# A two-layer hybrid transformer block: where the first feed-forward block of each stage puts its weights

## The chip, the cores and the metric

One core of a Trainium2 chip runs the whole kernel as one launch. The metric is the time of one execution on the device, in microseconds (us). TensorE is written PE, VectorE DVE, ScalarE ACT, GpSimd POOL and the engine that issues most of the DMAs SP.

## The reference

The input is 256 tokens of width 2048, in float32. Two layers follow each other. Layer 0 mixes with a gated delta rule and a gated linear recurrence, layer 1 with two kinds of attention; each mixer ends in an output projection that is added to the residual `h`. After each mixer comes the same feed-forward part, and the change is in it:

```
def swiglu(hn, w_gate, w_up, w_down):
    return (jax.nn.silu(hn @ w_gate) * (hn @ w_up)) @ w_down

def reference(...):
    h = x
    for layer in range(DEPTH):                      # 2
        h = h + mixer(rmsnorm(h, ...), ...)
        h = h + swiglu(rmsnorm(h, ffn_norm[layer]), ffn_w_gate[layer], ffn_w_up[layer], ffn_w_down[layer])
    return rmsnorm(h, final_norm)
```

`w_gate` and `w_up` are 2048 x 5632, `w_down` is 5632 x 2048.

## The kernel before, in words

Float32 products are made of two rounded halves. A weight tile `raw` of 128 x 1024 floats (512 KB) comes from memory; ACT casts it to the high half (`whi` or `thi`, line 608 in the feed-forward part, line 181 in the mixers), DVE subtracts that from `raw` and gets the low half (`wlo` or `tlo`, line 620, in the mixers line 182). PE then multiplies with the high and low halves of the activations `X`: high by high, high by low, low by high (lines 473 to 475).

There are four phases: mixer 0, feed-forward 0, mixer 1, feed-forward 1. Each phase opens pools of its own with `phase()` (lines 65 to 75), over the memory of the phase before. A tile in them can be written only when all that the earlier phase still reads in that memory is done. Pools `wr` (three buffers for `raw`), `wh` (four for `whi`), `wl` (three for `wlo`) and the accumulators in `acc` and `msp` stay through all phases. The phase's own `mx` pool gives further buffers for weights, two under each of the names `raw`, `ha`, `hb` and `hc`; its `fp` pool gives `thi` and `tlo` (two of each) and `comb`.

`ffn()` (line 720) cuts the work into blocks, eleven for the hidden columns (512 of gate and of up each) and six for the way down, and each block into steps (class `Step`, line 438). A plain step (`simple`, line 480) loads one 512 KB tile and uses it in 12 matmuls of 128 x 512. Other steps belong to a scheme with seven products in place of eight (`seven`, line 490); it holds tiles in `ha`, `hb`, `hc` and adds further weights to them with accumulating DMAs from POOL. The first block of each stage has no such products: it is sixteen plain steps, called step 0 to step 15 here. Steps with odd number use another pair of accumulators (F01, F11) than those with even number (F00, F10).

`stream()` (line 566) writes the steps out. `loads_to` (577) issues loads up to eight steps ahead as long as a buffer under the wanted name is promised free; `ahead` (597) writes the casts, `low` (615) the subtractions. Every sixth cast from step 1 and from step 4 goes to `thi`; the subtractions of steps 1 and 3 of every five go to `tlo`. What is written is then ordered for each engine by the framework's scheduler by when operands and buffers become free, up to the first step of the second block, from which the written order is kept (`guard`, line 628). SP issues the loads of all phases in one order: a load whose buffer isn't free holds back all behind it.

In the kernel before, the first ten steps of a stage ask in turn for `raw`, `ha`, `raw`, `hb`, `raw`, `hc` (lines 486 to 488), and of the loads that ask for `raw`, the first, third, sixth and so on get a buffer of the new `mx` pool and the others one of `wr` (line 592). Step 0 so loads to a new buffer, step 1 to `ha`, step 2 to `wr`.

Ahead of the stage stands the mixer's output projection (`xstat`, lines 305 to 307; `out_proj`, 356). After its last matmuls DVE adds the result to `h` in two halves of 128 tokens (line 361), ACT sums the squares of `h` into a scrap tile `junk` of the old mixer's memory (line 319), PE transposes `h` (line 328), ACT and DVE make the two halves of the last quarter of `X` (329, 330).

Of the kernel before, what the change touches and what calls it, by code (L numbers as in the profile page):

```python
# [4 lines left out]
F32, F32R, I32 = dt.float32, dt.float32r, dt.int32  # L5
# [42 lines left out]
def body(tc, A, out):  # L48
# [8 lines left out]
    wr = pool("wr", 3)  # L57
# [4 lines left out]
    mx, ogp, fp = Phase(), Phase(), Phase()  # L62
# [91 lines left out]
    def tick():  # L154

        count[0] += 1
        if paused[0]:
            return
        n = 0
        odd = not more and count[0] % 2  # L160
        for t in list(tasks)[::turns[0]]:
            if count[0] - t[0] >= t[2] and n < (2 if more else 4) and not (odd and t[2] > 1):
                step(t)
                n += 1
# [280 lines left out]
    class Mix:  # L445
# [34 lines left out]
        def simple(self, i, u, first):  # L480
            b = {}

            def use(w, tt=(0, 1)):
                for t in tt:
                    self.add(t, i, lambda kk: self.xs(2 * u + kk, t), w)
            k = 2 * u + i
            return Step(("raw", "ha", "raw", "hb", "raw", "hc")[k % 6] if first and k < 10 else "raw",
                        lambda raw: nc.sync.dma_start(raw, self.src(i, u)), use, unit=(i, use))

        def seven(self, m):  # L490
# [75 lines left out]
    def stream(order, puts, guard):  # L566

        at = [0, 0, 0]
        where = {id(y): k for k, y in enumerate(order)}
        g = None

        slots, count_raw = {}, [0]

        def loads_to(n, must=False):
            while at[2] < min(n, len(order)):
                y = order[at[2]]
                if y.tag:  # L580
                    q = slots.setdefault(y.tag, [])
                    if len(q) == (5 if y.tag == "raw" else 2):
                        k = where[id(q[0])]
                        if k >= at[1]:
                            if not must:
                                return
                            low(k)
                        q.pop(0)
                    q.append(y.free)
                    if y.tag == "raw":  # L590
                        count_raw[0] += 1
                    y.raw = (wr.tile([128, 1024], F32, name="raw") if y.tag == "raw" and count_raw[0] % 5 in (0, 2, 4) else
                             mx.tile([128, 1024], F32, name=y.tag, tag=y.tag, bufs=2))
                    y.load(y.raw)
                at[2] += 1

        def ahead(n):

            while at[0] < min(n + 1, len(order)):
                y, k = order[at[0]], at[0]  # L600
                loads_to(k + 1, True)
                for z in y.needs:
                    low(where[id(z)])
                if y.ready:
                    y.raw = y.ready()
                y.hi = (fp.tile([128, 1024], F32R, name="thi", tag="thi", bufs=2) if k % 6 in (1, 4) else
                        wh.tile([128, 1024], F32R, name="whi"))
                S.copy(y.hi, y.raw)  # L608
                at[0] += 1
                if at[0] > 1:  # L610
                    low(at[0] - 2)
            while at[1] < min(n, len(order)):
                low(at[1])

        def low(k):
            while at[1] <= k:
                y, j = order[at[1]], at[1]
                y.lo = (fp.tile([128, 1024], F32R, name="tlo", tag="tlo", bufs=2) if j % 5 in (1, 3) else
                        wl.tile([128, 1024], F32R, name="wlo"))
                V.tensor_sub(y.lo, y.raw, y.hi.bitcast(F32))  # L620
                at[1] += 1
                if y.after:
                    y.after()

        for n, y in enumerate(order):
            for f in puts.get(n, []):
                f()
            if y is guard:
                g = tc.manual_schedule(engines={V.engine, S.engine, PE.engine})
                g.__enter__()  # L630
            loads_to(n + 8)
            ahead(n + 1 + 3)
            y.use((y.hi, y.lo))
            if y.unit:
                tick()
        for n in sorted(k for k in puts if k >= len(order)):
            for f in puts[n]:
                f()
        if g is not None:
            g.__exit__(None, None, None)  # L640
# [79 lines left out]
    def ffn(L, then, fin=None):  # L720
# [120 lines left out]
        else:  # L841
            put(q + 2, lambda: then(0), lambda: then(1))
        stream(order, puts, blocks[1].early[0])

        if not fin:
# [757 lines left out]
```

## Time and profile before

| | |
|---|---|
| median of 3 runs | 2230.15 us (2229.86 to 2231.21) |
| the profiled execution | 2229.7 us |
| its span, first to last instruction | 2227.5 us |
| PE busy | 2203.5 us (99%) |
| DVE busy | 1829.3 us (82%) |
| ACT busy | 1341.4 us (60%) |
| DMA | 485.25 MB, 218 GB/s on average |
| mean granted PE clock | 0.996 |

The profile is one execution. "PE F L473 <- ACT whi L608" names an engine, what it wrote and the line, and who released it. In the chain of waits, the program is followed back from its last instruction, at each step to what released it, so its rows join end to start. In a timeline, the first column is the start in us from the span's start, the second the duration; a matmul's duration overlaps the next one's start, so the pace of PE is read from the starts. "SPq" is SP's queue of DMA issues. In the answers on DMAs the last column is the time from issue to landing.

### The profile page before, as it was taken

How to read it: one execution, taken by the hardware profiler on the slowest of the kernel's cores; microseconds unless marked ns; L12 is line 12 of the kernel's file. 1: busy time of each engine (PE TensorE's matmuls, PEld its weight loads, DVE VectorE, ACT ScalarE, POOL GpSimd, SP SyncE). 2: the span in 40 equal slices, each digit the busy share in tenths (PEclk: the TensorE clock that was granted, in tenths of full speed). 3: DMA queues.
4: the chain of work that ended last, by engine and by line, in shares of the span. 5: the costliest groups of instructions: out<-in, count | busy, mean ns of one | idle time of the engine just before them, and what ended most of it. 6: DMA issues, size and time to landing. Idle time of an engine off the chain costs nothing.

```text
span 2227.5 us, 30574 instructions
## 1 busy us (share of the span) xinstructions
PE 2203.5 (99%) x10960; PEld 1844.0 (83%) x10960; DVE 1829.3 (82%) x2554; ACT 1341.4 (60%) x1775; POOL 106.2 (5%) x126
## 2 busy tenths in 40 slices
PE   9999999999999999999999999999999999999998
PEld 8888888788888888888888888887888888888886
DVE  8899676679888888888786688857888888988886
ACT  6776664556665666666654554445665566665665
POOL 0000000000100000000000000000000100100000
PEclk9999999999999999999999999999999999999999
DMA  7445446687988888888555455566788887888884
GB/s 285 156 146 166 139 149 187 206 256 228 257 267 247 237 284 237 264 255 253 171 188 158 156 186 171 162 184 221 219 255 277 237 274 245 238 272 249 234 263 133
DMA packets 135209, 485.25 MB, mean 218 GB/s; under 512 B 15088, under 2 KB 16624, under 8 KB 134928
## 3 DMA queue, kind: packets, MB, share of 16 engines
q1 hardware_dynamic: 117488, 420.10, 54.6%
q0 software_dynamic: 17280, 62.92, 16.4%
q8 instruction: 86, 1.41, 0.3%
q14 instruction: 67, 0.55, 0.1%
q10 hardware_dynamic: 288, 0.27, 0.0%
HBM read 481.13 MB, written 2.10 MB: 217 GB/s over the span
## 4 chain that ended last, share of the span: by engine, by line
PE 97%; DVE 1%; DMA 1%; ACT 0%; issue 0%; DVEq 0%; ACTq 0%; SPq 0%
PE F L474 20%; PE F L473 20%; PE F L475 20%; PE Pw L201 11%; PE Pw L206 6%; PE Px L305 3%; PE Px L306 3%; PE Px L307 3%; PE F L420 1%; PE F L421 1%; PE Ph L735 1%; PE F L419 1%; PE Psc L1365 1%; PE Pw L247 0%; PE Pt L328 0%; PE Pw L248 0%
## 5 line engine op out<-in xcount | busy, mean ns | idle before, releaser
L181 ACT CAST whi<-raw 128x1024 fp32r<-128x1024 f32 x245 | 256.8, 1051 | 266.3 <-PE Pw L201 86.4
L182 DVE TENSOR_TENSOR wlo<-raw,whi 128x1024 fp32r<-128x1024 f32 x245 | 298.8, 1220 | 118.7 <-PE Px L306 37.7
L201 PE MATMUL Pw<-X,whi 128*128 128x512 f32 x1088 | 388.4, 400 | 0.0
L608 ACT CAST whi<-raw 128x1024 fp32r<-128x1024 f32 x238 | 249.4, 1054 | 109.9 <-PE F L475 88.1
L206 PE MATMUL Pw<-X,wlo 128*128 128x256 f32 x1088 | 304.8, 280 | 0.1
L473 PE MATMUL F<-whi,X 128*128 128x512 f32 x712 | 279.2, 393 | 9.9 <-ACT whi L608 9.9
L475 PE MATMUL F<-whi,X 128*128 128x512 f32 x712 | 278.2, 391 | 0.0
L608 ACT CAST whi<-ha 128x1024 fp32r<-128x1024 f32 x152 | 160.5, 1056 | 167.0 <-DVE ha L503 41.4
L201 PEld LDWEIGHTS Pw<-X,whi 128*128 128x128 f32 x1088 | 204.2, 188 | 47.2 <-issue 0.5
L474 PE MATMUL F<-wlo,X 128*128 128x512 f32 x588 | 230.4, 392 | 0.1
L206 PEld LDWEIGHTS Pw<-X,wlo 128*128 128x128 f32 x1088 | 205.4, 189 | 1.5 <-DVE wlo L182 0.7
L620 DVE TENSOR_TENSOR wlo<-raw,whi 128x1024 fp32r<-128x1024 f32 x140 | 170.3, 1219 | 4.6 <-ACT whi L608 0.9
L473 PEld LDWEIGHTS F<-whi,X 128*128 128x128 f32 x712 | 134.4, 189 | 37.9 <-ACT whi L608 10.4
L474 PE MATMUL F<-tlo,X 128*128 128x512 f32 x420 | 163.4, 389 | 0.0
L475 PEld LDWEIGHTS F<-whi,X 128*128 128x128 f32 x712 | 134.4, 189 | 27.9
L620 DVE TENSOR_TENSOR wlo<-ha,whi 128x1024 fp32r<-128x1024 f32 x96 | 117.4, 1222 | 37.4 <-ACT whi L608 25.6
L608 ACT CAST thi<-ha 128x1024 fp32r<-128x1024 f32 x92 | 97.3, 1057 | 76.4 <-DVE ha L503 32.6
L474 PEld LDWEIGHTS F<-wlo,X 128*128 128x128 f32 x588 | 111.2, 189 | 24.4 <-DVE wlo L620 1.5
L473 PE MATMUL F<-whi,hid 128*128 128x512 f32 x336 | 131.2, 390 | 0.0
L475 PE MATMUL F<-whi,hid 128*128 128x512 f32 x336 | 130.8, 389 | 0.0
L608 ACT CAST thi<-raw 128x1024 fp32r<-128x1024 f32 x100 | 105.2, 1052 | 36.7 <-PE F L475 32.1
L474 PE MATMUL F<-wlo,hid 128*128 128x512 f32 x320 | 124.5, 389 | 0.0
(444 smaller groups left out, 4887.8 us busy)
## 6 DMA issues: line engine op xcount, KB each, us to landing
raw<-in_gu SPq DMA_DIRECT2D x222, 512.0 KB, 5.5
raw<-in_dn SPq DMA_DIRECT2D x116, 512.0 KB, 4.9
raw<-in_w0w SPq DMA_DIRECT2D x72, 512.0 KB, 3.7
raw<-in_wo SPq DMA_DIRECT2D x64, 512.0 KB, 3.7
raw<-in_w1w SPq DMA_DIRECT2D x64, 512.0 KB, 3.7
ha<-in_gu SPq DMA_DIRECT2D x44, 512.0 KB, 5.2
hb<-in_gu SPq DMA_DIRECT2D x44, 512.0 KB, 7.6
hc<-in_gu SPq DMA_DIRECT2D x42, 512.0 KB, 5.6
```

Of the source, the lines that this page charges most:

```text
L181: S.copy(hi, raw)
L182: V.tensor_sub(lo, raw, hi.bitcast(F32))
L201: PE.matmul(P.rearrange("p a b -> p (a b)"), hi[:, kk], X[:, k].rearrange("p a b -> p (a b)"), start=k == 0, stop=False)
L206: PE.matmul(P[:, 0], lo[:, kk], X[:, k, 0], start=False, stop=k == NK - 1)
L305: PE.matmul(Ps[t], x[:, 0, ts], hi[:, kk], start=k == 0, stop=False)
L306: PE.matmul(Ps[t], x[:, 0, ts], lo[:, kk], start=False, stop=False)
L307: PE.matmul(Ps[t], x[:, 1, ts], hi[:, kk], start=False, stop=k == n - 1)
L473: PE.matmul(P, xh, hi[:, kk], start=z[0] == 1 and kk == 0, stop=False, skip_group_check=skip)
L474: PE.matmul(P, xh, lo[:, kk], start=False, stop=False, skip_group_check=skip)
L475: PE.matmul(P, xl, hi[:, kk], start=False, stop=kk == 1 and z[0] in z[1:], skip_group_check=skip)
L608: S.copy(y.hi, y.raw)
L620: V.tensor_sub(y.lo, y.raw, y.hi.bitcast(F32))
```

## The change: what it does

All steps of a stage's first block now carry the name `first`, and such a load always gets one of the three `wr` buffers. Other plain loads take turns between `wr` and `mx` as before, with a counter of their own (`turn`), and the bookkeeping of promised buffers is kept for each pool of buffers apart (`wr` 3, and 2 each of `raw`, `ha`, `hb`, `hc`) rather than five for `raw` together. Nothing is computed otherwise, and each engine has the same instructions as before.

```diff
-            k = 2 * u + i
-            return Step(("raw", "ha", "raw", "hb", "raw", "hc")[k % 6] if first and k < 10 else "raw",
+            return Step("first" if first else "raw",
                         lambda raw: nc.sync.dma_start(raw, self.src(i, u)), use, unit=(i, use))
...
-        slots, count_raw = {}, [0]
+        slots, turn = {}, [0]
+        bufs = dict(wr=3, raw=2, ha=2, hb=2, hc=2)
...
-                    q = slots.setdefault(y.tag, [])
-                    if len(q) == (5 if y.tag == "raw" else 2):
+                    wide = y.tag == "raw" and turn[0] % 5 in (1, 3)
+                    tag = y.tag if wide or y.tag in bufs and y.tag != "raw" else "wr"
+                    q = slots.setdefault(tag, [])
+                    if len(q) == bufs[tag]:
...
-                    if y.tag == "raw":
-                        count_raw[0] += 1
-                    y.raw = (wr.tile([128, 1024], F32, name="raw") if y.tag == "raw" and count_raw[0] % 5 in (0, 2, 4) else
-                             mx.tile([128, 1024], F32, name=y.tag, tag=y.tag, bufs=2))
+                    turn[0] += y.tag == "raw"
+                    y.raw = (wr.tile([128, 1024], F32, name="raw") if tag == "wr" else
+                             mx.tile([128, 1024], F32, name=tag, tag=tag, bufs=bufs[tag]))
```

The line numbers below the first edit grow by one or two: the cast of line 608 stands in line 609 after the change, the subtraction of line 620 in line 621, the load of line 488 in 487, that of line 499 in 498.

The order of the instructions changes on every engine around the start of both feed-forward stages, in the same way at both. The three pieces below are from the first one.

SP, from the last loads of mixer 0's output projection on, before. L488 is a plain step's load, L499 one of the seven-product steps of the second block:

```order
L175 DMA raw<-in_wo 128x1024 x32
L488 DMA raw<-in_gu 128x1024 x4
L488 DMA ha<-in_gu 128x1024
L488 DMA hb<-in_gu 128x1024
L488 DMA raw<-in_gu 128x1024
L488 DMA hc<-in_gu 128x1024
L488 DMA ha<-in_gu 128x1024
L488 DMA hb<-in_gu 128x1024
L488 DMA raw<-in_gu 128x1024 x2
L499 DMA ha<-in_gu 128x1024
```

The same place on SP after the change (L487 a plain load, L498 one of the second block):

```order
L175 DMA raw<-in_wo 128x1024 x32
L487 DMA raw<-in_gu 128x1024 x5
L498 DMA ha<-in_gu 128x1024 x2
L498 DMA hb<-in_gu 128x1024
L487 DMA raw<-in_gu 128x1024 x3
L498 DMA hb<-in_gu 128x1024
L498 DMA hc<-in_gu 128x1024
L487 DMA raw<-in_gu 128x1024 x3
L498 DMA hc<-in_gu 128x1024
L487 DMA raw<-in_gu 128x1024 x3
```

Before, the first three loads go to `wr` (they are those of steps 2, 6 and 8), the fourth is step 0's, to the new memory. After, the first five are steps 0 to 4 in their order, all to `wr`, and three loads of the second block, to the new memory, stand ahead of step 5's.

ACT around the end of the mixer, before. The x4 at L329 make a quarter of `X`; `junk` is the sum of squares; L399 is a cast for the seven-product scheme:

```order
L181 CAST whi<-raw 128x1024 x2
L319 ACTIVATE junk,ssp<-h 128x512 x2
L329 ACTIVATE X<-Pt,col 128x256 x4
L319 ACTIVATE junk,ssp<-h 128x512 x2
L329 ACTIVATE X<-Pt,col 128x256 x4
L608 CAST whi<-raw 128x1024 x2
L608 CAST thi<-ha 128x1024
```

And after the change:

```order
L181 CAST whi<-raw 128x1024 x2
L319 ACTIVATE junk,ssp<-h 128x512 x2
L609 CAST whi<-raw 128x1024
L329 ACTIVATE X<-Pt,col 128x256 x4
L609 CAST whi<-raw 128x1024 x2
L319 ACTIVATE junk,ssp<-h 128x512 x2
L329 ACTIVATE X<-Pt,col 128x256 x4
L609 CAST thi<-raw 128x1024 x2
L399 CAST comb<-cc_4740 128x1024
```

Three casts, those of steps 0, 2 and 3, moved ahead of the last sum of squares; step 1's and step 4's, to `thi`, follow the last quarter of `X`. DVE's subtractions of steps 0 and 2 moved in the same manner ahead of the last additions to `h`.

PE at the same place, before. F_4654 and F_4661 are the accumulators F00 and F10:

```order
L307 MATMUL Px_4489<-whi,Od 128x512
L328 MATMUL Pt<-tab,h 128x128 x8
L473 MATMUL F_4654<-whi,X 128x512
L473 MATMUL F_4661<-whi,X 128x512
L474 MATMUL F_4654<-wlo,X 128x512
L475 MATMUL F_4654<-whi,X 128x512
```

And after the change, where F00 is F_4648:

```order
L307 MATMUL Px_4489<-whi,Od 128x512
L473 MATMUL F_4648<-whi,X 128x512
L328 MATMUL Pt<-tab,h 128x128 x4
L474 MATMUL F_4648<-wlo,X 128x512
L328 MATMUL Pt<-tab,h 128x128 x4
L475 MATMUL F_4648<-whi,X 128x512
L473 MATMUL F_4648<-whi,X 128x512
```

Step 0's matmuls now start between the mixer's last matmul and the eight last transposes. Behind step 0 come two matmuls of step 2, then two of step 1, six of step 2, ten of step 1 and four of step 2, and then step 3, 4, 5 and so on in turn.

## The prediction

> **What bounds the kernel now.** I read the busy times, then the chain that ended last, then PE's waits.
>
> ```profile
> PE 2203.5 (99%) x10960; PEld 1844.0 (83%) x10960; DVE 1829.3 (82%) x2554; ACT 1341.4 (60%) x1775; POOL 106.2 (5%) x126
> PE 97%; DVE 1%; DMA 1%; ACT 0%; issue 0%; DVEq 0%; ACTq 0%; SPq 0%
> PE F L473 <- ACT whi L608: 9.9, 2, 5.0
> ```
>
> PE is busy 99% of the span and carries 97% of the chain. Little is left to win, 24 us of idle time, and 9.9 us of that are two waits of 5 us for a cast. They stand at the two starts of the feed-forward part, where the change is. The chain through the first start, and the load in the chain at the second:
>
> ```profile
> 429.91 0.24 PE Px L307
> ...
> 430.17 0.70 DVE h L361
> ...
> 430.96 0.64 ACT junk L319 x2
> ...
> 431.64 0.72 ACT junk L319 x2
> ...
> 432.39 3.56 DMA raw<-in_gu
> ...
> 436.03 1.05 ACT whi L608
> ...
> 437.12 1.22 PE F L473 x2
> ```
> ```profile
> 1523.79 3.74 DMA raw<-in_gu
> ```
>
> The mixer's last matmul is followed by the addition to `h`, the sum of squares into `junk`, a load of 3.56 us, a cast of 1.05 us, and only then step 0's matmuls. The load has to wait for `junk` because its buffer lies in memory that the mixer still uses. The granted clock, in stretches from the end of the mixer's last matmul on:
>
> ```profile
> 430.67:437.12 6.45, 1.46 (x9) 0.76 0.59 191
> 437.12:440.88 3.76, 3.71 (x8) 0.51 1.02 416
> 1522.07:1528.70 6.63, 1.45 (x9) 0.82 0.57 187
> 1528.70:1533.27 4.57, 4.53 (x10) 0.52 1.01 407
> ```
>
> After the gap PE runs for 3.8 and 4.6 us at a clock of 0.51 and 0.52 (fifth column). So each start costs an idle stretch and a slow one. How long the start takes as a whole is read from PE's timeline:
>
> ```profile
> 423.87 0.39 PE L306 MATMUL Px<-wlo,Od 128*128 128x512 f32 x1
> ...
> 427.48 0.39 PE L306 MATMUL Px<-wlo,Od 128*128 128x512 f32 x1
> ...
> 430.43 0.39 PE L307 MATMUL Px<-whi,Od 128*128 128x512 f32 x1
> ...
> 444.62 0.39 PE L473 MATMUL F<-whi,X 128*128 128x512 f32 x1
> ...
> 447.34 0.39 PE L473 MATMUL F<-whi,X 128*128 128x512 f32 x1
> ...
> 1521.83 0.39 PE L307 MATMUL Px<-whi,Om 128*128 128x512 f32 x1
> ...
> 1539.24 0.39 PE L473 MATMUL F<-whi,X 128*128 128x512 f32 x1
> ```
> ```profile
> 424.49 0.87 PE Pt L328 x8
> ```
>
> A step is 12 matmuls; step 2 runs from 444.62 to 447.34, 2.72 us, 0.227 a matmul. The mixer's last matmul starts at 430.43 and is through at 430.66; step 3 starts at 447.34. That is 16.68 us for steps 0 to 2 and eight transposes. At the second start it is 1522.06 to 1539.24, 17.18 us. The work itself is 3 x 2.72 = 8.16 us and 0.87 us of transposes, 9.03 us. So 7.65 and 8.15 us are lost, 15.8 in all, and no more than that can be won here.
>
> **The change, first part: the loads start earlier.** SP's issues before:
>
> ```profile
> 417.42 0.33 SPq L488 DMA_DIRECT2D raw<-in_gu  x1
> 420.25 2.96 SPq L488 DMA_DIRECT2D raw<-in_gu  x2
> 432.39 0.33 SPq L488 DMA_DIRECT2D raw<-in_gu  x1
> ```
> ```profile
> raw<-in_gu SPq DMA_DIRECT2D x1, 512.0 KB, 3.5
> ```
>
> At 417.42, 420.25 and 422.88 (the end of the second row, less 0.33) the three `wr` buffers are refilled, with steps 2, 6 and 8. Now the same three issues bring steps 0, 1 and 2, and by 3.5 to 3.6 us each they are there at 421, 424 and 426.5. What ACT and DVE do around that:
>
> ```profile
> 424.74 1.57 ACT L329 ACTIVATE X<-Pt,col 128x256 fp32r<-128x256 f32 x4 [3.16 <-PE Pt L328]
> ...
> 432.27 1.55 ACT L329 ACTIVATE X<-Pt,col 128x256 fp32r<-128x256 f32 x4
> ...
> 437.93 1.04 ACT L608 CAST thi<-ha 128x1024 fp32r<-128x1024 f32 x1
> ```
> ```profile
> 421.63 1.23 DVE L182 TENSOR_TENSOR wlo<-raw,whi 128x1024 fp32r<-128x1024 f32 x1 [0.80 <-ACT junk L319]
> ...
> 430.17 1.37 DVE L361 TENSOR_TENSOR h<-Px,h 128x512 f32<-128x512 f32 x2 [3.27 <-PE Px L307]
> 432.40 1.23 DVE L407 TENSOR_TENSOR cf<-X 128x1024 f32<-128x1024 f32 x1 [0.85 <-ACT junk L319]
> 433.54 1.66 DVE L330 SCALAR_TENSOR_TENSOR X<-Pt,col,X 128x256 fp32r<-128x256 f32 x4
> 435.11 0.75 DVE L396 TENSOR_TENSOR cc<-cf 128x256 f32<-128x256 f32 x2
> ...
> 436.57 0.16 DVE L340 TENSOR_SCALAR rx<-rx 128x2 f32<-128x2 f32 x1
> ...
> 440.52 1.22 DVE L401 TENSOR_TENSOR comb<-cc,comb 128x1024 fp32r<-128x1024 f32 x1
> ```
>
> Step 0 is cast about 422 to 423, when the mixer's `whi` of four tiles back is free; its subtraction waits for `wlo` of three tiles back, whose last matmul (L306 at 423.87) ends at 424.3, and is done by 425.5. That frees the first buffer: step 3's load, issued at 425.6, lands at 429.2 and is cast by 430.3. Step 2 is cast by 427.6, ahead of `junk`, and subtracted when the mixer's next `wlo` falls free at 427.9 (L306 at 427.48), by 429.15. That frees the buffer for step 4, which lands at 432.8. All of it lies in idle time of ACT and DVE: ACT's 3.16 us before 424.74, DVE's 3.27 us before 430.17. It delays neither `h` at 430.17 nor `junk` at 430.96; the nearest thing is step 3's cast, with 0.6 us in hand.
>
> **Second part: PE's order.** Both halves of step 0 being there, PE goes from the mixer's last matmul at 430.66 into step 0's first one. The transposes of the first half need `h` at 430.87, those of the second at 431.54, and with a matmul between them each has only some 0.1 us to wait; so step 0 and the transposes end at 430.66 + 2.72 + 0.87 + 0.15 = 434.4. Two matmuls of step 2 follow, to 434.85. Step 1's high half goes to `thi`, in new memory, and so its cast can only follow `junk` and the last quarter of `X`: 432.27 + 1.55 = 433.8, and with 1.04 us of cast it is there at 434.85, just when PE asks for it. Its subtraction stands behind the last L330 on DVE, which ends at 435.1, and is done at 436.3; PE has two matmuls of step 1 and six of step 2 to do until 436.7. Steps 1 and 2 end at 434.4 + 2 x 2.72 = 439.88.
>
> **Third part: what is late next.** From step 3 on a load waits for the subtraction three steps back. DVE does steps 3 and 4 by 437.4 and 438.6, PE starts them at 439.88 and 442.6. Step 5's load waits for step 1's buffer until 436.3, and on SP it stands behind two `ha` and one `hb`, which have waited for `junk` until 432.39 as step 0's load did before. What a pile on the queue costs, from the seven loads that were issued between 432.39 and 435.52, is in the last column (the fourth and the last of them):
>
> ```profile
> raw<-in_gu SPq DMA_DIRECT2D x1, 512.0 KB, 6.8
> hb<-in_gu SPq DMA_DIRECT2D x1, 512.0 KB, 9.4
> ```
>
> The fourth, issued at 433.71, lands at 440.5, the seventh, at 435.52, at 444.9: 1.5 us for each load in the pile. Three loads from 432.4 on are through by 439, so step 5 lands at about 440.2 and its cast could be done at 441.3. On DVE, though, four operations on `cc` and two small ones (435.11 to 436.73, 1.6 us), one on `cf` (1.2) and one on `comb` (1.2) stand between step 4's subtraction and step 5's, so that this one ends at 438.6 + 4.0 + 1.2 = 443.8. PE asks for it with the second matmul of step 5, 439.88 + 5.44 + 0.23 = 445.55: 1.75 us in hand. By the same count step 8's low half is there at 451.8, needed at 453.7, step 11's at 457.9, needed at 461.9. No wait is left. The queue also carries the second block's tiles, but these are issued earlier than before.
>
> **The sum.** Steps 0 to 2 end at 439.88 and not at 447.34: 7.46 us. At the second start the same 9.22 us take the place of 17.18: 7.96 us. Together 15.4 us. In other terms: the idle time goes, 5.56 + 5.74 us (437.12 - 430.66 and 1528.70 - 1522.06, less 0.9 of transposes each), and so does what the low clock costs, 10.22 - 8.16 = 2.06 and 10.54 - 8.16 = 2.38 us, less 0.3 us of small waits. All that follows is bound by PE, so the gain should reach the end. The profiled execution, at 2229.7 us, becomes 2214.3; the median of the runs is 0.45 us above it, and the forecast is 2214.8 us.
>
> The slow stretch is the term that rests least on counting. The Trainium skill ("TensorE: Matmul & The Clock Gate", part "What's actually happening") says that PE falls to half its clock after an idle window of about 3.4 us and comes back after as long a busy one. By that the slow stretch costs half of 3.4 us, 1.7 us at each start, and the sum would be 14.4 us; the trace has 2.06 and 2.38, and I go by the trace.
>
> **Rivals.** *The ring of three is a little late.* If each of the loads of steps 5, 8 and 11 took as long as the median `hb`,
>
> ```profile
> hb<-in_gu SPq DMA_DIRECT2D x44, 512.0 KB, 7.6
> ```
>
> step 5's would land at 436.3 + 7.6 = 443.9, its low half would be there at 446.25 (0.7 us late), and each round of three steps would take 7.6 + 1.05 + 1.2 + 0.1 = 9.95 us of load, cast and subtraction against PE's 8.16: 1.8 us more at steps 8 and 11 each, some 4.2 us at each start. The gain would be 15.4 - 8.4 = 7 us, the time 2222 to 2223. For it speaks that the second block's loads share the queue; against, that they are few and lone loads take 3.5 us. Chance 0.14.
>
> *Slower: starvation.* The same ring becomes a loss where a load takes 8.8 us in each of three rounds (4.2 + 3 x 1.2 = 7.8 us at a start); at the 9.4 us of the row above it would be 4.2 + 5.4 = 9.6 us against a gain of 7.7, so 3.8 us slower in all, 2234; if the gaps pulled the clock down again, more. For: such a landing is in the trace, and SP is in order. Against: it belonged to seven loads issued in 3.6 us, and a ring of three can't pile up so. Chance 0.06.
> The Trainium skill's "DMA: Bandwidth & Descriptors" (part "Rules for kernel authors") speaks on this side: issue a DMA early and wait late, so that its fixed cost overlaps. Before, nine loads could be ahead; now three are, and no run here shows yet what that costs.
>
> *No change.* The new order could be held by something else that falls free only with `junk`, such as `thi`: step 1 stands in the sum with no time in hand. But even were all of PE to wait for it, steps 0 and 2 would be done meanwhile. Only if step 0 also waited until 437 would the time stay at 2230. Chance 0.04.
>
> **Numbers.** The forecast has 0.76: 2213.5 (all 15.8 us, and the runs' 0.7 us) to 2219 (up to 2 us lost again at each start). The range reaches into the first rival, to 2222. Faster by over 0.2% (4.5 us, about what a measurement of this kernel can tell from none) are the forecast and the first rival, 0.90; same 0.04; slower 0.06.
>
> **What would show it.** Right: the 9.9 us of PE's wait for the cast at its two places are gone, PE's clock stays at 1.0 there, and step 3 starts 9.2 us after the mixer's last matmul. Wrong: PE waits for L609 or L621 at steps 4 to 8, with landings of 7 us or more in the ring; or a wait for `thi` at step 1; or the gain is there at 450 us and gone at the second block.

## The result and the profile after

The changed kernel takes 2214.84 us (median of 4 runs, 2214.37 to 2215.07), the kernel before, run beside it, 2230.6 us (2229.86 to 2231.21). The ratio is 0.9929, 95% interval 0.9912 to 0.9946. The profiled execution took 2214.64 us, its span 2212.8 us.

The busy times and the shares of the chain, after:

```profile
PE 2198.9 (99%) x10960; PEld 1842.3 (83%) x10960; DVE 1827.9 (83%) x2554; ACT 1339.6 (61%) x1775; POOL 105.9 (5%) x126
PE 98%; DVE 1%; ACT 0%; DMA 0%; issue 0%; DVEq 0%; ACTq 0%
```

PE's waits, all that the view lists, after:

```profile
PE Pz L92 <- ACT tab L89: 2.7, 1, 2.7
PE Pgate L950 <- ACT cx L887: 0.6, 1, 0.6
PE Pt L328 <- DVE X L330: 0.4, 1, 0.4
```

The two waits of 5 us for a cast are gone and nothing has come in their place; what is left was there before. PE's timeline at the first start, after, from the mixer's last matmul to step 3's first one:

```profile
431.02 0.39 PE L307 MATMUL Px<-whi,Od 128*128 128x512 f32 x1
431.25 0.39 PE L473 MATMUL F<-whi,X 128*128 128x512 f32 x1
431.51 0.66 PE L328 MATMUL Pt<-tab,h 128*128 128x128 f32 x4
431.93 0.47 PE L474 MATMUL F<-wlo,X 128*128 128x512 f32 x1
432.24 0.61 PE L328 MATMUL Pt<-tab,h 128*128 128x128 f32 x4
...
435.43 0.64 PE L473 MATMUL F<-thi,X 128*128 128x512 f32 x2
...
440.43 0.39 PE L473 MATMUL F<-whi,X 128*128 128x512 f32 x1
```

And PE in the stretches of steps 0 to 2 at both starts, after (busy time, granted clock, share of the DMA engines, GB/s):

```profile
431.25:440.43 9.18, 9.18 (x45) 1.00 0.68 220
1514.86:1524.04 9.18, 9.18 (x46) 1.00 0.81 282
```

Step 0 follows the mixer's last matmul without a gap, and steps 0 to 2 with the eight transposes take 9.18 us at each start, at full clock, where they took 16.68 and 17.18 us. That is 7.50 + 8.00 = 15.5 us, against 15.8 us between the medians.

### The profile page after: what moved, and what is told of

Its sections match the earlier page's. It is cut to its first block, busy times and chain, and to the rows that moved or that the text cites. A ratio compares the mean times of both kernels' runs of the same rounds, so it can differ in the third digit from the quotient of the medians.

```text
span 2212.8 us, 30570 instructions
## 1 busy us (share of the span) xinstructions
PE 2198.9 (99%) x10960; PEld 1842.3 (83%) x10960; DVE 1827.9 (83%) x2554; ACT 1339.6 (61%) x1775; POOL 105.9 (5%) x126
## 4 chain that ended last, share of the span: by engine, by line
PE 98%; DVE 1%; ACT 0%; DMA 0%; issue 0%; DVEq 0%; ACTq 0%
PE F L474 20%; PE F L475 20%; PE F L473 20%; PE Pw L201 11%; PE Pw L206 6%; PE Px L305 3%; PE Px L307 3%; PE Px L306 3%; PE F L421 1%; PE F L420 1%; PE F L419 1%; PE Ph L736 1%; PE Psc L1366 1%; PE Pt L328 0%; PE Pw L247 0%; PE Pw L248 0%
## 5 line engine op out<-in xcount | busy, mean ns | idle before, releaser
L181 ACT CAST whi<-raw 128x1024 fp32r<-128x1024 f32 x245 | 256.8, 1051 | 264.2 <-PE Pw L201 86.1
L182 DVE TENSOR_TENSOR wlo<-raw,whi 128x1024 fp32r<-128x1024 f32 x245 | 298.8, 1220 | 119.3 <-PE Px L306 37.9
L609 ACT CAST whi<-raw 128x1024 fp32r<-128x1024 f32 x244 | 255.5, 1053 | 102.6 <-PE F L475 72.6
L473 PE MATMUL F<-whi,X 128*128 128x512 f32 x712 | 277.8, 390 | 0.0
L621 DVE TENSOR_TENSOR wlo<-raw,whi 128x1024 fp32r<-128x1024 f32 x144 | 175.2, 1218 | 9.7 <-PE Px L306 3.0
L473 PEld LDWEIGHTS F<-whi,X 128*128 128x128 f32 x712 | 133.7, 188 | 27.3
L473 PE MATMUL F<-whi,hid 128*128 128x512 f32 x336 | 131.2, 390 | 0.0
L621 DVE TENSOR_TENSOR tlo<-raw,whi 128x1024 fp32r<-128x1024 f32 x100 | 121.9, 1219 | 7.2 <-ACT whi L609 4.4
```

The source lines that it names most:

```text
L181: S.copy(hi, raw)
L182: V.tensor_sub(lo, raw, hi.bitcast(F32))
L473: PE.matmul(P, xh, hi[:, kk], start=z[0] == 1 and kk == 0, stop=False, skip_group_check=skip)
```

## The experiments

Three theories were at stake. **A**: step 0's load waits for memory that the mixer's sums of squares still hold; PE idles until its cast, and the low clock after the gap costs more. **B**: the gain comes from the shorter queue and the small ring, not from where the first tiles lie. **C**: the slow stretch belongs to the first steps whatever PE did before. The kernel before stands at 2231.2 us beside e1, e3, e5 and e6 and at 2231.16 us beside e2, e4 and e7. Beside each time the table has the length from the start of the mixer's last matmul to the start of the second block's first matmul with a combined operand (L473, F<-whi,comb), at both starts, from the profiled execution: it holds the first block whole.

| kernel | us, median | ratio to before, interval | first start, us | second start, us |
|---|---|---|---|---|
| before | 2230.6 to 2231.2 | | 46.8 | 47.3 |
| after | 2214.84 | 0.9929 [0.9912, 0.9946] | 39.3 | 39.3 |
| e1: of steps 0 to 2, step 0 in an old buffer | 2225.72 | 0.9974 [0.9964, 0.9984] | 45.6 | 44.6 |
| e2: first stage alone | 2222.76 | 0.9965 [0.9952, 0.9978] | 39.4 | 48.3 |
| e3: gap filled | 2228.22 | 0.9987 [0.9978, 0.9997] | 46.5 | 45.9 |
| e4: the change for steps 0 to 4 only | 2214.53 | 0.9928 [0.9912, 0.9945] | 39.4 | 39.4 |
| e5: scrap tile moved | 2214.61 | 0.9922 [0.9907, 0.9937] | 39.3 | 39.3 |
| e6: ring of two | 2229.01 | 0.9986 [0.9976, 0.9995] | 45.3 | 46.2 |
| e7: 4 and 3 fillers | 2230.48, one run | | 47.0 | 48.7 |

**e5: the wait's cause taken away, the buffers of before.**

```diff
-                 mx.tile([128, 512], F32, name="junk", tag="t2", bufs=4))
+                 res.tile([128, 512], dt.bfloat16, name="junk", tag="junk", bufs=1))
```

> Before, with the same buffers for all steps (nine loads ahead, step 0 into the new memory); only the mixers' scrap tile for the sums of squares is moved into memory of its own that lives through all phases (in bfloat16, since it is never read). That frees the new phase's memory well before the mixer ends. Theory A: the loads go out during the mixer's last matmuls and the whole gain is there without the change, 2215 us (2214 to 2217). Theory B (the order of the queue or the small ring is what helps): 2228 to 2231 us. That the memory is held by more than the scrap tile: PE's wait is shorter, by no more than a few us.

2214.61 us: the whole gain, without the change. PE's waits in e5, the first rows:

```profile
PE Pz L92 <- ACT tab L89: 2.7, 1, 2.7
PE Pgate L949 <- ACT cx L886: 0.6, 1, 0.6
PE Pt L328 <- DVE X L330: 0.4, 1, 0.4
PE F L420 <- DVE tlo L379: 0.3, 1, 0.3
```

The 5 us ones are gone, and the first block is as short as after. So nine loads ahead and step 0 in new memory do no harm once that memory is free in time: B falls, and the scrap tile was all that held the start back.

**e1: one early step moved.** The shift by one gives the `wr` buffers to steps 0, 4 and 6, where before they went to steps 2, 6 and 8.

```diff
-        slots, count_raw = {}, [0]
+        slots, count_raw = {}, [1]
```

> Before, with the rotation of the weight buffers shifted by one, so that of a stage's first three steps only step 0 loads into an old buffer (steps 1 and 2 still go to the new phase's memory). Theory A (a step's load waits for the new memory; PE idles until its cast, and the clock falls in long gaps): step 0 fills PE to about 4 us after the mixer's last matmul, then PE idles some 3.3 us at each start for step 1, whose load can only go out after the sums of squares. 2214.8 + 2 x 3.3 = 2221.4 us if so short a gap leaves the clock alone, 2225.5 us if the clock falls as before. Theory B (the gain comes from the new order of queue and ring, three loads in place of nine, and not from the place of the first tiles): nearly all of the gain is missing, 2229 us or more.

2225.72 us, the value that A gives if the clock falls. PE's timeline at the first start, with the end of step 0 and the first matmuls of step 1, and the clock in the gap and behind it:

```profile
433.90 0.39 PE L475 MATMUL F<-whi,X 128*128 128x512 f32 x1
437.24 1.22 PE L473 MATMUL F<-thi,X 128*128 128x512 f32 x2 [2.94 <-ACT thi L608]
```
```profile
434.27:437.24 2.97, 0.03 (x2) 0.86 0.87 268
437.24:443.13 5.89, 5.85 (x13) 0.50 1.02 410
```

Step 0 fills PE to 434.3; then it waits 2.94 us for step 1, and runs 5.9 us at half clock. So of the first three steps one in an old buffer gets a third of the gain (5.5 of 15.8 us). The first five steps are enough:

**e4: the small ring only for five steps.**

```diff
-            return Step("first" if first else "raw",
+            return Step("first" if first and 2 * u + i < 5 else "raw",
```

> After, but only steps 0 to 4 of a stage's first block are bound to the three old buffers; steps 5 to 15 take turns between old and new buffers, five in all. Theory A (the ring of three costs nothing, all its halves are there in time, the nearest by 0.6 us): 2214.8 us, within 0.5. Rival (the ring of three gives back a part of the gain): 2212 to 2213.5 us, and more time in hand at step 5's low half.

2214.53 us, no different from after. The low half that was nearest to late, step 5's, has more time in hand at the first start here: its subtraction on DVE, and the first matmul that reads it on PE, in e4 (one row of each engine's timeline):

```profile
442.19 1.23 DVE L621 TENSOR_TENSOR wlo<-raw,whi 128x1024 fp32r<-128x1024 f32 x1
```
```profile
445.40 0.39 PE L474 MATMUL F<-wlo,X 128*128 128x512 f32 x1
```

It is done at 443.42 and asked for at 445.40. After the change itself the same two rows are:

```profile
444.23 1.23 DVE L621 TENSOR_TENSOR wlo<-raw,whi 128x1024 fp32r<-128x1024 f32 x1 [1.24 <-ACT whi L609]
```
```profile
446.10 0.39 PE L474 MATMUL F<-wlo,X 128*128 128x512 f32 x1
```

445.46 against 446.10: 0.64 us in hand, where e4 has 1.98. At the second start after itself has as much as e4 at the first:

```profile
1526.51 1.22 DVE L621 TENSOR_TENSOR wlo<-raw,whi 128x1024 fp32r<-128x1024 f32 x1
```
```profile
1529.71 0.39 PE L474 MATMUL F<-wlo,X 128*128 128x512 f32 x1
```

It is done at 1527.73 and asked for at 1529.71, 1.98 us later. So the ring of three costs no time, and that it costs time in hand isn't shown: the 0.64 us stand at one start of one execution.

**e6: a ring of two.** The buffer is held by a read on DVE that also needs the low half of step 11:

```diff
+        hold = wr.tile([128, 1024], F32, name="raw")
+        V.memset(hold[:, 0:1], 0.0)
...
-                    if len(q) == bufs[tag]:
+                    if len(q) == (2 if y.tag == "first" else bufs[tag]):
...
+        put(p0[11], lambda: V.tensor_tensor(out=mx.tile([128, 1], F32, name="hd", tag="hd", bufs=1), in0=hold[:, 0:1], in1=order[p0[11]].lo[:, 0:1].bitcast(F32), op=ALU.add))
```

> After, but one of the three old buffers is kept occupied until step 11, so the first block has a ring of two. Theory A with the ring as priced: two steps take PE 5.44 us, a round of load (4 to 6 us), cast and subtraction 6.5 to 8.4 us, so PE waits from step 4 on, 1 to 3 us in each round, some 7 us at each start: 2229 us (2223 to 2240), PE's waits on L609 and L621. If the ring doesn't matter at all: 2214.8 us.

2229.01 us, as priced: 6.0 and 6.9 us longer at the two starts than after. PE's timeline at its first wait, and the clock behind it:

```profile
447.12 0.74 PE L473 MATMUL F<-thi,X 128*128 128x512 f32 x2 [1.63 <-ACT thi L609]
448.38 0.80 PE L474 MATMUL F<-wlo,X 128*128 128x512 f32 x1 [0.52 <-DVE wlo L621]
...
461.85 0.50 PE L474 MATMUL F<-tlo,X 128*128 128x512 f32 x1 [0.47 <-DVE tlo L621]
```
```profile
449.20:451.50 2.30, 2.30 (x6) 0.50 0.88 249
```

This is the starving rival, with one buffer less: waits for the cast and the low half at step 4 and on, and one gap pulls the clock down. It takes back most of the gain. The price of 7 us a start was one of waits alone; the waits that the view lists come to 3.0 us from 440 to 470 us, and the slow stretch behind the first of them (3.4 us at half clock, 448.40 to 451.80), which wasn't in the price, makes up a part of the rest. So three buffers suffice here, and two do not.

**e3: the gap filled, the wait left.**

```diff
+        Pd = acc.tile([128, 512], F32, name="Pq", tag="acc")
+        for _ in range(5):
+            PE.matmul(Pd, tb["ident"], h[:, 1, 1536:2048], start=True, stop=True)
```

> Before, with five float32 matmuls of 128 x 512 that nobody reads put into PE's gap at both starts (identity times the last quarter of h, so they can't start before h is there); the output stays the reference's. PE's wait for the first weights stays, only PE is busy meanwhile. Theory A: the low clock after the gap goes, 2.06 + 2.38 us, 2230.6 - 4.4 = 2226.2 us; the granted clock in the first 4 us of step 0 is near 1.0. Rival C (the slow stretch is part of the start of the steps, whatever PE did before): 2230.6 us or more, and the clock stays near 0.5.

2228.22 us, 3.0 us faster; the ratio's interval allows 0.7 to 4.9 us. The clock at both starts, in the first 4 us of step 0:

```profile
439.07:443.07 4.00, 3.48 (x13) 1.00 0.91 334
1530.27:1534.27 4.00, 3.47 (x14) 1.00 1.02 413
```

It stays at 1.0, so C falls: the slow stretch comes from the gap. But the starts are only 0.4 and 1.4 us shorter in this execution, not 2.06 and 2.38. Where the rest stays, PE's timeline at the second start of e3 shows:

```profile
1530.27 0.73 PE L473 MATMUL F<-whi,X 128*128 128x512 f32 x2 [0.76 <-ACT whi L608]
1531.53 0.50 PE L474 MATMUL F<-wlo,X 128*128 128x512 f32 x1 [0.53 <-DVE wlo L620]
```

Two matmuls start at 1530.27 and the third, which reads the low half, at 1531.53: 1.26 us where the pace would give 0.45. In the kernel before it was the same 1.26 us (437.12 to 438.38):

```profile
437.12 1.22 PE L473 MATMUL F<-whi,X 128*128 128x512 f32 x2 [4.87 <-ACT whi L608]
438.38 0.79 PE L474 MATMUL F<-wlo,X 128*128 128x512 f32 x1
```

So 0.8 us at each start, which the prediction put under the clock, are a wait for DVE's subtraction after the cast. At the first start of e3 a further matmul waits for step 1's low half (0.40 us).

**e2: one stage alone.** The second stage gets the names and the rotation of before. In its trace SP, PE, ACT and DVE do the same things in the same order around the second start as in the kernel before, so the new bookkeeping by itself moves nothing there.

```diff
-            return Step("first" if first else "raw",
+            k = 2 * u + i
+            return Step(("raw", "ha", "raw", "hb", "raw", "hc")[k % 6] if first == 2 and k < 10 else "first" if first == 1 else "raw",
...
-        slots, turn = {}, [0]
+        slots, turn = {}, [shift]
...
-                            *space, first=b == 0)
+                            *space, first=(1 if L == 0 else 2) if b == 0 else 0)
...
-        stream(order, puts, blocks[1].early[0])
+        stream(order, puts, blocks[1].early[0], 1 if (1 if L == 0 else 2) == 2 else 0)
```

> The change for the first feed-forward stage alone; the second one has the buffers of before. Theory A (each start has its own loss, 7.5 and 8.0 us, and nothing is given back later): 2214.8 + 8.0 = 2222.8 us on the scale of the first comparison, PE's one wait of 5 us left at the second start. Rival (the two starts aren't independent, or the gain of the first is lost in mixer 1): more than 2225 us or less than 2220.

2222.76 us, with one wait of 5.0 us left on PE. The two starts are separate, and nothing is given back in mixer 1.

**e7: shorter gaps.** The edit is that of e3 with four fillers at the first start and three at the second.

> Before, with PE's gap filled by four of the unread float32 matmuls at the first start and three at the second, which leaves gaps of about 1.5 and 2.4 us. It asks how long a gap pulls the clock down. By the runs so far a gap of 1.6 us with 0.5 us behind it was followed by a slow stretch and one of 1.4 with 0.5 was not: so the second start should show a clock near 0.5 for 3 to 4 us, the first may go either way. If only gaps of 3.4 us or more count, both starts stay at 1.0. One look; its time, about 2229 us, decides nothing.

PE's timeline at the two starts, and the clock behind the gaps:

```profile
436.40 0.73 PE L473 MATMUL F<-whi,X 128*128 128x512 f32 x2 [1.30 <-ACT whi L608]
...
1528.07 0.73 PE L473 MATMUL F<-whi,X 128*128 128x512 f32 x2 [2.41 <-ACT whi L608]
```
```profile
436.40:440.40 4.00, 3.45 (x13) 1.00 1.00 382
1529.33:1533.33 4.00, 4.00 (x9) 0.50 1.02 414
```

After a gap of 1.30 us the clock stays; after one of 2.41 us it falls to half, some 0.6 us after PE has started again. The gap at the first start is one of those that the expectation left open.

## Why the prediction was right

- **The first loads go out earlier, and step 0 is ready when the mixer ends.** Shown: step 0's first matmul starts 0.23 us after the mixer's last one starts. That the held memory was the cause is shown by e5; that, as long as it is held, the place of the first tiles decides, by e1.
- **Steps 0 to 2 in 9.22 us.** 9.18 us at both starts. The two transposes' waits and the wait for `thi` are as small as counted: step 1's first matmul, just in time in the count, starts at 435.43 without one.
- **Nothing is late next.** True, at the first start with less in hand than counted. The count had step 5's load land at 440.2, 1.75 us to spare for its low half; with this execution's mixer ending 0.6 us later, that is 440.8. SP's timeline after, and the one load issued from 436.5 to 437.2 with its time to landing:

```profile
433.30 1.74 SPq L498 DMA_DIRECT2D ha<-in_gu  x1
435.09 0.42 SPq L498 DMA_DIRECT2D hb<-in_gu  x1
436.88 0.33 SPq L487 DMA_DIRECT2D raw<-in_gu  x1
```
```profile
raw<-in_gu SPq DMA_DIRECT2D x1, 512.0 KB, 6.2
```

It was issued when the count had it, but took 6.2 us to land where the count had 3.9. It landed at 443.1, and 0.64 us were left. The `ha` ahead of it took 1.74 us to issue, where the seven issues of before that the count went by took 0.3 to 0.7 us; whether that made the landing late isn't shown. At the second start the same load landed in 4.5 us and 1.98 us were left, close to the 1.75 us of the count. So at the first start the first rival, a ring that is a little late, was near; a ring of two is over the edge.
- **Idle 11.3 us and clock 4.4 us.** The sum is right, the split is not. Of the 4.4 us some 1.6 us are the wait for the low half behind the first cast, which PE at half clock only partly covers, and e3 puts the clock's own part at 3.0 us by the medians and at 1.8 us by its trace. It made no difference here, because the change removes both.
- **The gain reaches the end.** 15.8 us between the medians, 15.5 us at the two starts; e2 splits it as counted. That forecast and median agree within 0.04 us is luck: the runs after the change spread over 0.7 us.

## What to carry to other kernels

Where a phase opens memory over the one before, look which late and trivial access of the old phase holds it: here a scrap tile that nobody reads kept the next phase's first weight out until the very end, and moving it (e5) is worth as much as rerouting the loads. Give the first few loads buffers that live through both phases; five were enough, and the ring behind them must be counted in load, cast and subtraction against PE's time for as many steps. A gap on an engine that is busy 99% costs more than its length: count the low clock behind it, and the waits that the low clock was hiding.

## What the runs showed of the hardware

The clock falls after shorter gaps than expected. Gaps of 2.94, 2.54, 2.41 and 1.63 us (e1 at both starts, e7, e6; the last three with 0.5 us of waiting soon behind) were followed by half clock, gaps of 1.37, 1.30 and 0.76 us (the second start of e6, the first of e7, the second of e3, each with 0.5 us behind it) were not. The Trainium skill ("TensorE: Matmul & The Clock Gate", part "What's actually happening") puts the fall after an idle window of about 3.4 us; these runs have it after less, and the measurement decides.

The length of the gap is not all. In slices of 0.05 us, the clock of e1 falls at 436.40 us at the first start, within the gap, and at 1528.65 at the second, 1.75 us after the gap has ended at 1526.90. In the 3.41 us before each of these falls PE was busy for less than half the time (second column the length, third the busy time):

```profile
432.99:436.40 3.41, 1.30 (x6) 1.00 0.82 229
1525.24:1528.65 3.41, 1.22 (x4) 1.00 1.02 410
```

Read in the same way, the half clock lasts 3.4 us (e1's second start, to 1532.10; e6, 448.40 to 451.80) or 6.8 us (before, 434.00 to 440.80 and 1526.25 to 1533.10; e1, 436.40 to 443.25; e2, 1522.60 to 1529.45; e7, 1528.70 to 1535.50), idle time included. The shorter stretches agree with the busy window of about 3.4 us that the same section of the Trainium skill has, and the longer ones are twice that. So the 3.8 and 4.6 us of slow work in the kernel before are the rest of stretches that began in the gap. This looks as if the clock were set anew every 3.4 us by how busy PE had been, so that what a short gap costs would depend on when it comes; that is inferred from these figures, and no run tests it.
